# A row-tiled matmul with bias and residual: eight row tiles to a super tile, one listed order of transfers, and bf16 pairs transposed as words

## The chip, the cores and the metric

The kernel runs on one core of a Trainium2 chip. The metric is the device time of one execution in microseconds (us). Three runs of the kernel before gave a median of 217.84 us (216.41 to 219.18). The engines are named as in the profile: PE is TensorE's matmul stream and PEld its weight loads, DVE is VectorE, ACT is ScalarE, POOL is GpSimd, SP is SyncE, which issues nearly all transfers; a q behind a name (SPq, PEq) is that engine's queue of instructions.

## The reference

```python
batch, m, k, n = 16, 512, 1024, 768      # all float32
def reference(x, weight, bias, residual):
    return (np.matmul(x, weight) + bias + residual).astype(np.float32)
```

With the batch flattened it is one matmul of 8192 x 1024 by 1024 x 768, with a row of bias and a residual of the output's shape added. x is 33.6 MB, the residual and the output 25.2 MB each, the weight 3.1 MB: 87 MB to move.

## The kernel before, in words

**Tiling.** The 8192 rows are cut into 64 row tiles of 128 rows, and `J = 4` row tiles make a super tile S of 512 rows. Within a super tile, partition p holds J rows that follow each other in memory, so one transfer of x for a super tile is 2 MB, 16 KB in one piece for each partition; for the residual and the output it is 1.5 MB, 12 KB each. Row tile t is slice `t % 4` of super tile `t // 4`.

**One row tile** goes through these steps:

- `cast(t)` (L92): ACT turns the f32 x tile (128 x 1024) into the bf16 tile `xb`.
- `transp(t)` (L98 and L100): PE transposes the eight 128 x 128 blocks of `xb` into the PSUM tile `pt`, and DVE copies `pt` to `xt` in SBUF.
- `mm(t, k, n0, nl)` (L103): for each of the eight blocks k of the contraction and each of two column chunks (512 and 256) one bf16 matmul into the PSUM tile `psum_o`, 16 in all. Block k of W holds the rows 128k to 128k + 127.
- `finish(t)` and `pool_add(t)`: for the first eight tiles (`EARLY = 8`) DVE adds bias to the product into one of four `tmp` tiles (L122) and POOL adds that to the residual in `ro` (L114). For all later tiles POOL adds the bias to the residual row beforehand (L114), and DVE adds the product to that row (L124).

**Loop.** For t from 3 to 63 (L187), in program order: the cast of tile t + 2, at the last tile of a super tile the loads of x (S + 3), of the residual (S + 2) and the store of S - 1, the transposes of tile t + 1, the 16 matmuls of tile t, the finishing add of tile t - 1, and POOL's bias add of tile t + 1. Each engine keeps this order.

**Head.** `HEAD_ORDER` (L20) interleaves the loads of x tiles 0 to 2 and of the eight W chunks (each 128 x 768, 384 KB). When an x tile arrives it is cast, transposed and multiplied with the W chunks seen so far; when a W chunk arrives DVE casts it to bf16 (L164) and it is multiplied with the x tiles seen so far. Ahead of that stand eleven warming matmuls of 512 columns (L141), the load of the bias row on POOL's queue (L128), and two f32 matmuls of a row of ones with the bias row (L146) that spread the bias over the partitions, which DVE copies to `bias_sb` (L151).

**Buffers and queues.** x has three slots of a super tile, `ro` seven, of which the last two first hold the f32 W chunks. All loads and stores but the bias row's are issued by SP, in program order; one that waits for its slot or for its data holds up all behind it.

**Tail.** The last super tile is stored in parts: two row tiles, one, and the last one in its two column chunks, each after its own add (L205 to L212).

Of the kernel before, what the change touches and what calls it, by code (L numbers as in the profile page):

```python
# [19 lines left out]
HEAD_ORDER = [  # L20
    ("x", 0), ("w", 0), ("x", 1), ("w", 1), ("w", 2), ("x", 2),
    ("w", 3), ("w", 4), ("w", 5), ("w", 6), ("w", 7),
]


@with_exitstack
def kernel(
    ctx: ExitStack,
    tc: tile.TileContext,
    x: bass.AP,  # L30
    weight: bass.AP,
    bias: bass.AP,
    residual: bass.AP,
    out: bass.AP,
):
# [6 lines left out]
    n_k = K // P  # L42
# [9 lines left out]
    const = ctx.enter_context(tc.tile_pool(name="const", bufs=1))  # L52
# [3 lines left out]
    def ring(pool, name, i, n, shape, dt):  # L56
        return pool.tile(shape, dt, name=name, tag=f"{name}{i % n}", bufs=1)

    def psum_o(i):
        return ring(ps, "psum_o", i, HEAD, [P, N], FP32)  # L60

    x_sb, ro, xb, xt, po, tmp = {}, {}, {}, {}, {}, {}
    K_ = tc.keep_in_program_order

    def load_x(S, j0=0, j1=J):
        if S < n_s:
            if j0 == 0:
                x_sb[S] = ring(sb, "x_tile", S, X_BUFS, [P, J, K], FP32)
            K_(nc.sync.dma_start(out=x_sb[S][:, j0:j1, :], in_=x_d[S, :, j0:j1, :]))

    def load_res(S, j0=0, j1=J):
        if S < n_s:
            if j0 == 0:
                ro[S] = ring(sb, "ro", S, RO_BUFS, [P, J, N], FP32)
            K_(nc.sync.dma_start(out=ro[S][:, j0:j1, :], in_=res_d[S, :, j0:j1, :]))

    def store(S, j0=0, j1=J, n0=0, nl=N):
        if 0 <= S < n_s:
            K_(nc.sync.dma_start(
                out=out_d[S, :, j0:j1, n0:n0 + nl], in_=ro[S][:, j0:j1, n0:n0 + nl]  # L80
            ))

    w_st = [
        ring(sb, "ro", RO_BUFS - 2 + h, RO_BUFS, [P, n_k // 2, N], FP32) for h in range(2)
    ]
    w_sb = const.tile([P, n_k, N], BF16, name="w_sb")


    def cast(t):
        if t < n_t:  # L90
            xb[t] = ring(sb, "xb", t, 4, [P, K], BF16)
            K_(nc.scalar.copy(out=xb[t], in_=x_sb[t // J][:, t % J, :]))  # L92

    def transp(t):
        if t < n_t:
            pt = ring(ps, "pt", t, 2, [P, n_k, P], BF16)
            for k in range(n_k):
                K_(nc.tensor.transpose(out=pt[:, k, :], in_=xb[t][:, ts(k, P)], identity=ident))  # L98
            xt[t] = ring(sb, "xt", t, 4, [P, n_k, P], BF16)
            K_(nc.vector.tensor_copy(out=xt[t], in_=pt))  # L100

    def mm(t, k, n0, nl):
        K_(nc.tensor.matmul(  # L103
            po[t][:, n0:n0 + nl], lhsT=xt[t][:, k, :], rhs=w_sb[:, k, n0:n0 + nl],
            start=(k == 0), stop=(k == n_k - 1),
        ))

    def row(t, n0=0, nl=N):
        return ro[t // J][:, t % J, n0:n0 + nl]

    def pool_add(t):
        if t < n_t:
            r = row(t)
            K_(nc.gpsimd.tensor_add(out=r, in0=r, in1=tmp[t] if t < EARLY else bias_sb))  # L114

    def finish(t, n0=0, nl=N):
        if t < 0:
            return
        p = po[t][:, n0:n0 + nl]
        if t < EARLY:  # L120
            tmp[t] = ring(sb, "tmp", t, TMP_BUFS, [P, N], FP32)
            K_(nc.vector.tensor_add(out=tmp[t], in0=p, in1=bias_sb))  # L122
        else:
            K_(nc.vector.tensor_add(out=row(t, n0, nl), in0=p, in1=row(t, n0, nl)))  # L124


    bias_row = const.tile([1, N], FP32, name="bias_row")
    K_(nc.gpsimd.dma_start(out=bias_row, in_=bias[None, :]))  # L128
    warm = const.tile([P, 512], BF16, name="warm")
    K_(nc.vector.memset(warm, 0.0))  # L130
    ones_row = const.tile([1, P], FP32, name="ones_row")
    K_(nc.vector.memset(ones_row, 1.0))
    warm_a = const.tile([1, 2], FP32, name="warm_a")
    K_(nc.vector.memset(warm_a, 0.0))
    K_(nc.scalar.copy(out=warm_a, in_=warm_a))  # L135
    ident = const.tile([P, P], BF16, name="ident")
    make_identity(nc, ident)

    warm_ps = psum_o(0)
    for _ in range(WARM_MM):  # L140
        K_(nc.tensor.matmul(  # L141
            warm_ps[:, 0:512], lhsT=warm[:, 0:P], rhs=warm, start=True, stop=True
        ))
    bias_ps = psum_o(HEAD - 1)
    for n0, nl in chunks:
        K_(nc.tensor.matmul(  # L146
            bias_ps[:, n0:n0 + nl], lhsT=ones_row, rhs=bias_row[:, n0:n0 + nl],
            start=True, stop=True,
        ))
    bias_sb = const.tile([P, N], FP32, name="bias_sb")  # L150
    K_(nc.vector.tensor_copy(out=bias_sb, in_=bias_ps))  # L151


    seen_x, seen_w = [], []
    for kind, i in HEAD_ORDER:
        if kind == "x":
            load_x(0, i, i + 1)
            cast(i)
            transp(i)
            po[i] = psum_o(i)  # L160
            seen_x.append(i)
        else:
            K_(nc.sync.dma_start(out=w_st[i // 4][:, i % 4, :], in_=w_d[:, i, :]))
            K_(nc.vector.tensor_copy(out=w_sb[:, i, :], in_=w_st[i // 4][:, i % 4, :]))  # L164
            seen_w.append(i)
        for t in seen_x if kind == "w" else [i]:
            for k in [i] if kind == "w" else seen_w:
                for n0, nl in chunks:
                    mm(t, k, n0, nl)
    load_x(0, 3, 4)  # L170
    load_x(1, 0, 2)
    load_res(0, 0, 2)
    load_x(1, 2, 4)
    load_res(0, 2, 4)
    load_x(2)
    load_res(1)
    cast(HEAD)
    transp(HEAD)
    cast(HEAD + 1)
    load_x(3)  # L180
    load_res(2)
    for t in range(HEAD - 1):
        finish(t)
        pool_add(t)


    for t in range(HEAD, n_t):  # L187
        cast(t + 2)
        if (t + 2) % J == J - 1:
            S = (t + 2) // J  # L190
            load_x(S + X_BUFS)
            load_res(S + 2)
            store(S - 1)
        transp(t + 1)
        po[t] = psum_o(t)
        if t < n_t - 1:
            for k in range(n_k):
                for n0, nl in chunks:
                    mm(t, k, n0, nl)
# [5 lines left out]
    S = n_s - 1  # L205
    store(S, 0, J - 2)
    store(S, J - 2, J - 1)
    for n0, nl in chunks:
        for k in range(n_k):
            mm(n_t - 1, k, n0, nl)  # L210
        finish(n_t - 1, n0, nl)
        store(S, J - 1, J, n0, nl)  # L212


# [28 lines left out]
```

## Time and profile before

| what | value |
|---|---|
| three runs, median (lowest, highest) | 217.84 us (216.41, 219.18) |
| span of the profiled execution, first to last instruction | 216.1 us; the profile gives no time around it |
| mean granted TensorE clock | 0.975 of full speed |
| moved by DMA | 87.28 MB, mean 404 GB/s |
| HBM read, written | 61.87 MB, 25.17 MB |
| POOL waiting for residual loads | 60.8 us in 14 waits |
| ACT waiting for PE's transposes (slots of `xb`) | 102.8 us in 52 waits |
| ACT waiting for x loads | 24.2 us in 8 waits |

How to read it: the rows that the prediction quotes come from views of one profiled execution. The page shows each engine's busy time, and then the span in 40 equal slices (5.4 us each) with a digit of busy tenths. The chain that ended last lists start, duration and what was done. A group of instructions is a line, an engine, an operation and its operands, then the count, the busy time in us and the mean ns of one, then the idle time ahead of it and what ended that. A busy time of PE or PEld is not the distance from one instruction to the next, since they overlap. In the view by stretches, DMA share is the mean busy share of the core's 16 DMA engines, and the number ahead of it the granted clock.

### The profile page before, as it was taken

The page shows a single profiled execution, that of the slowest core. Times are in us where ns is not written, and L with a number is a line of the kernel's source. Part 1 is how long each engine was busy: PE and PEld are TensorE (multiplying, and loading weights), DVE is VectorE, ACT ScalarE, POOL GpSimd, SP SyncE. Part 2 cuts the span into 40 slices and gives each one's busy share as a digit, 9 for nine tenths or more (in the row PEclk, how much of TensorE's full clock was granted, in tenths as well). Part 3 has the DMA queues.
Part 4 walks back from the last instruction along what each step waited for, and adds up shares of the span by engine and source line. Part 5 has one row for each costly group of instructions (what it writes and reads, how often), then busy time and mean ns, then how long its engine had stood idle before and what let it go on. Part 6 is the DMA issues. An engine that isn't in the chain of part 4 may idle for free.

```text
span 216.1 us, 3672 instructions
## 1 busy us (share of the span) xinstructions
PE 205.2 (95%) x1551; PEld 132.4 (61%) x1551; DVE 105.1 (49%) x141; ACT 68.0 (31%) x66; POOL 115.3 (53%) x71
## 2 busy tenths in 40 slices
PE   7678799999999999999999999999999999999992
PEld 2335566666666666666666666666666666666651
DVE  0245365445554455445544555445544555445542
ACT  2314416323332333323332333323332333231000
POOL 2000096669928467390928457290936629099600
PEclk9658999999999999999999999999999999999999
DMA  6999999999999999999999999999999999999654
GB/s 179 393 413 418 441 413 429 428 425 431 428 422 431 425 427 421 434 422 421 440 418 436 426 432 420 431 428 422 434 417 438 421 432 424 434 414 416 260 233 176
DMA packets 9265, 87.28 MB, mean 404 GB/s; under 512 B 1056, under 2 KB 1184, under 8 KB 3360
## 3 DMA queue, kind: packets, MB, share of 16 engines
q1 hardware_dynamic: 9216, 87.04, 96.0%
q8 instruction: 12, 0.20, 0.4%
q14 instruction: 5, 0.04, 0.0%
q0 software_dynamic: 32, 0.00, 0.0%
HBM read 61.87 MB, written 25.17 MB: 403 GB/s over the span
## 4 chain that ended last, share of the span: by engine, by line
PE 93%; DVE 3%; DMA 3%; issue 1%; DVEq 0%; POOLq 0%
PE psum_o L103 78%; PE pt L98 13%; DMA bias_row<-in_bias_dram 3%; PE psum_o L146 1%; DVE xt L100 1%; DVE ro L124 1%; DVE tmp L122 0%; DVE bias_sb L151 0%; DVE w_sb L164 0%; DVEq L124 0%; DVEq L100 0%; POOLq L227 0%; POOLq masks.py:199 0%
## 5 line engine op out<-in xcount | busy, mean ns | idle before, releaser
L103 PE MATMUL psum_o<-w_sb,xt 128*128 128x256 bf16 (+1 forms) x1024 | 178.8, 328 | 4.9 <-DVE xt L100 1.6
L103 PEld LDWEIGHTS <-xt 128*128 128x128 bf16 x1024 | 97.8, 98 | 64.9 <-issue 2.2
L114 POOL TENSOR_TENSOR ro<-ro,bias_sb 128x768 f32<-128x768 f32 x56 | 99.7, 1812 | 59.5 <-DMA ro<-in_residual_dram 59.5
L92 ACT CAST xb<-x_tile 128x1024 bf16<-128x1024 f32 x64 | 66.5, 1046 | 127.0 <-PE pt L98 102.8
L100 DVE COPY xt<-pt 128x1024 bf16<-128x1024 bf16 x64 | 44.3, 692 | 94.6 <-PE pt L98 94.6
L124 DVE TENSOR_TENSOR ro<-psum_o,ro 128x768 f32<-128x768 f32 (+2 forms) x57 | 53.3, 935 | 4.9 <-PE psum_o L103 3.0
L98 PEld LDWEIGHTS <-xb 128*128 128x128 bf16 x512 | 34.9, 100 | 9.1 <-ACT xb L92 0.7
L98 PE MATMUL pt<-ident,xb 128*128 128x128 bf16 x512 | 40.1, 223 | 0.0
L114 POOL TENSOR_TENSOR ro<-ro,tmp 128x768 f32<-128x768 f32 x8 | 14.4, 1811 | 27.7 <-DVE tmp L122 26.3
L122 DVE TENSOR_TENSOR tmp<-psum_o,bias_sb 128x768 f32<-128x768 f32 x8 | 7.5, 948 | 0.0
L141 PE MATMUL psum_o<-warm 128*128 128x512 bf16 x11 | 3.9, 531 | 1.2 <-DVE warm L130 1.2
L151 DVE COPY bias_sb<-psum_o 128x768 f32<-128x768 f32 x1 | 1.0, 958 | 8.0 <-PE psum_o L146 8.0
L164 DVE CAST w_sb<-ro 128x768 bf16<-128x768 f32 x8 | 4.0, 553 | 0.0
L146 PE MATMUL psum_o<-bias_row,ones_row 1*128 1x512 f32 (+1 forms) x4 | 2.3, 720 | 1.7 <-DMA bias_row<-in_bias_dram 1.7
L141 PEld LDWEIGHTS <-warm 128*128 128x128 bf16 x11 | 1.3, 129 | 3.3 <-issue 1.9
L146 PEld LDWEIGHTS psum_o<-bias_row,ones_row 1*128 1x128 f32 x4 | 0.9, 234 | 3.0 <-issue 3.0
L135 ACT ACT_TABLE_LOAD x1 | 1.3, 1283 | 0.7 <-PEq L227 0.7
L128 POOL DMA_DIRECT2D bias_row<-in_bias_dram x1 | 0.6, 646 | 0.8 <-POOLq L227 0.8
L130 DVE MEMSET warm<- 128x256 uint32 x1 | 0.3, 272 | 0.9 <-PEq L227 0.9
masks.py:199 POOL TENSOR_SCALAR_AFFINE_SELECT ident<-ident 128x128 bf16<-128x128 bf16 x1 | 0.3, 292 | 0.1
L227 POOL MEMSET const-float32-0.0<- 128x1 f32 x1 | 0.1, 98 | 0.2 <-issue 0.2
masks.py:197 POOL MEMSET ident<- 128x128 bf16 x1 | 0.2, 224 | 0.0
(6 smaller groups left out, 0.7 us busy)
## 6 DMA issues: line engine op xcount, KB each, us to landing
x_tile<-in_x_dram SPq DMA_DIRECT2D x14, 2048.0 KB, 24.5
ro<-in_residual_dram SPq DMA_DIRECT2D x15, 1536.0 KB, 27.8
out_dram<-ro SPq DMA_DIRECT2D x15, 1536.0 KB, 25.3
ro<-in_weight_dram SPq DMA_DIRECT2D x8, 384.0 KB, 8.5
x_tile<-in_x_dram SPq DMA_DIRECT2D x4, 512.0 KB, 7.2
x_tile<-in_x_dram SPq DMA_DIRECT2D x2, 1024.0 KB, 11.2
ro<-in_residual_dram SPq DMA_DIRECT2D x2, 768.0 KB, 11.7
out_dram<-ro SPq DMA_DIRECT2D x1, 768.0 KB, 3.3
```

What stands on the lines that cost most here:

```text
L92: K_(nc.scalar.copy(out=xb[t], in_=x_sb[t // J][:, t % J, :]))
L98: K_(nc.tensor.transpose(out=pt[:, k, :], in_=xb[t][:, ts(k, P)], identity=ident))
L100: K_(nc.vector.tensor_copy(out=xt[t], in_=pt))
L103: K_(nc.tensor.matmul(po[t][:, n0:n0 + nl], lhsT=xt[t][:, k, :], rhs=w_sb[:, k, n0:n0 + nl], start=(k == 0), stop=(k == n_k - 1),))
L114: K_(nc.gpsimd.tensor_add(out=r, in0=r, in1=tmp[t] if t < EARLY else bias_sb))
L122: K_(nc.vector.tensor_add(out=tmp[t], in0=p, in1=bias_sb))
L124: K_(nc.vector.tensor_add(out=row(t, n0, nl), in0=p, in1=row(t, n0, nl)))
L135: K_(nc.scalar.copy(out=warm_a, in_=warm_a))
L141: K_(nc.tensor.matmul(warm_ps[:, 0:512], lhsT=warm[:, 0:P], rhs=warm, start=True, stop=True))
L146: K_(nc.tensor.matmul(bias_ps[:, n0:n0 + nl], lhsT=ones_row, rhs=bias_row[:, n0:n0 + nl], start=True, stop=True,))
L151: K_(nc.vector.tensor_copy(out=bias_sb, in_=bias_ps))
L164: K_(nc.vector.tensor_copy(out=w_sb[:, i, :], in_=w_st[i // 4][:, i % 4, :]))
```

## The change

Six things change together.

1. `J` goes from 4 to 8. A super tile is 1024 rows; a transfer of x is 4 MB (32 KB per partition), of the residual or output 3 MB (24 KB per partition).
2. All SBUF and PSUM tiles are made once, as lasting slots: two for x, four for the residual and output (`R`), four each for `xb` and `xt`. The f32 W chunks first use slot 1 of `R`, and the early tiles' temporary results slot 3.
3. All transfers but the bias row's stand in one list, `ORDER`. The function `pump` issues, on SP, each entry of the list as soon as the program has written the instructions that it depends on; it is called after every step that could allow one more. The order of the list is the order on SP.
4. W is laid out so that partition p of a pair chunk q holds the rows 256q + 2p and 256q + 2p + 1. The bf16 tile `xb` is read as f32 words, each a pair of neighbouring bf16 values; PE transposes four blocks of 128 x 128 words in place of eight of bf16, with an f32 identity. The matmuls then take every second bf16 element of `xt` as their weights. The number and shape of the matmuls stay.
5. The head is written out in `HEAD_ORDER`: the two casts of each pair of x tiles run on DVE and ACT, the two halves of each W chunk likewise, and each W chunk is multiplied with tiles 0 to 2 when it comes; tile 3 is transposed in the head too. There are 24 warming matmuls of 256 columns in three groups. The bias row is loaded by ACT's queue.
6. Only the first six tiles go through a temporary result, and POOL's adds follow a list `ADDS` for the first 16 tiles. The last tile's two column chunks go to two PSUM tiles, and it is stored in one transfer.

The diff, cut to its core:

```diff
-J = 4
+J = 8
+X_SLOTS = 2
+RO_SLOTS = 4
 HEAD = 3
-X_BUFS = 3
-RO_BUFS = 7
-TMP_BUFS = 4
-EARLY = 8
-WARM_MM = 11
+WARM = 10
+EARLY_END = 6
+TMP_SLOT = {0: 3}
+ADDS = [6, 0, 7, 8, 1, 9, 2, 10, 3, 11, 4, 12, 5, 13, 14, 15]
+HEAD_ORDER = [('bias',), ('warm', 10), ('cast', 0, 'v'), ('cast', 1, 's'), ('tr', 0), ('tr', 1),
+ ('wc', 0, 0, 's'), ('wc', 0, 1, 'v'), ('warm', 4), ('mm', 0, 0), ('mm', 1, 0),
+ ('cast', 2, 'v'), ('cast', 3, 's'), ('tr', 2), ('tr', 3), ('wc', 1, 0, 's'), ('wc', 1, 1, 'v'),
+ ('mm', 2, 0), ('mm', 0, 1), ('mm', 1, 1), ('mm', 2, 1), ('wc', 2, 0, 's'), ('wc', 2, 1, 'v'),
+ ('mm', 0, 2), ('mm', 1, 2), ('mm', 2, 2), ('wc', 3, 0, 's'), ('wc', 3, 1, 'v'),
+ ('cast', 4, 's'), ('mm', 0, 3), ('mm', 1, 3), ('mm', 2, 3)]
+ORDER = [('x', 0, 0, 2), ('w', 0, 0, 2), ('x', 0, 2, 4), ('w', 1, 0, 2), ('w', 2, 0, 2), ('w', 3, 0, 2),
+ ('x', 0, 4, 6), ('x', 0, 6, 8), ('r', 0, 0, 5), ('x', 1, 0, 4), ('r', 0, 5, 8), ('r', 1, 0, 5),
+ ('x', 1, 4, 8), ('x', 2, 0, 8), ('r', 1, 5, 8), ('r', 2, 0, 8), ('x', 3, 0, 8), ('s', 0, 0, 8),
+ ('r', 3, 0, 8), ('x', 4, 0, 8), ('r', 4, 0, 8), ('s', 1, 0, 8), ('x', 5, 0, 8), ('r', 5, 0, 8),
+ ('s', 2, 0, 8), ('x', 6, 0, 8), ('r', 6, 0, 8), ('s', 3, 0, 8), ('x', 7, 0, 8), ('r', 7, 0, 8),
+ ('s', 4, 0, 8), ('s', 5, 0, 8), ('s', 6, 0, 8), ('s', 7, 0, 5), ('s', 7, 5, 7),
+ ('s', 7, 7, 8)]
...
-    w_d = weight.rearrange("(ko ki) n -> ki ko n", ki=P)
+    w_d = weight.rearrange("(q p e) n -> p q e n", p=P, e=2)
...
+    XT = fixed(sb, "xt", XT_N, [P, n_q, P, 2], BF16)
+    PT = fixed(ps, "pt", 2, [P, n_q, P], FP32)
+    (ident,) = fixed(sb, "ident", 1, [P, P], FP32)
...
+    def pump():
+        while queue:
+            kind, S, j0, j1 = queue[0]
+            if kind == "w":
+                need = []
+            elif kind == "x":
+                need = [("cast", J * (S - X_SLOTS) + j) for j in range(j0, j1)] if S >= X_SLOTS else []
+            elif kind == "r":
+                need = [("store", S - RO_SLOTS, j) for j in range(j0, j1)] if S >= RO_SLOTS else []
...
+            else:
+                need = [("out", J * S + j) for j in range(j0, j1)]
+            if not all(n in done for n in need):
+                return
...
     def transp(t):
         if t < n_t:
-            pt = ring(ps, "pt", t, 2, [P, n_k, P], BF16)
-            for k in range(n_k):
-                K_(nc.tensor.transpose(out=pt[:, k, :], in_=xb[t][:, ts(k, P)], identity=ident))
-            xt[t] = ring(sb, "xt", t, 4, [P, n_k, P], BF16)
-            K_(nc.vector.tensor_copy(out=xt[t], in_=pt))
+            words = XB[t % XB_N].bitcast(FP32)
+            pt = PT[t % 2]
+            for q in range(n_q):
+                K_(nc.tensor.transpose(out=pt[:, q, :], in_=words[:, ts(q, P)], identity=ident))
+            K_(nc.vector.tensor_copy(
+                out=XT[t % XT_N].rearrange("p q m e -> p (q m e)"),
+                in_=pt.rearrange("p q m -> p (q m)").bitcast(BF16),
+            ))
...
+            PO[t % HEAD][:, n0:n0 + nl], lhsT=XT[t % XT_N][:, q, :, e],
+            rhs=w_sb[:, q, e, n0:n0 + nl],
...
-    K_(nc.gpsimd.dma_start(out=bias_row, in_=bias[None, :]))
+    K_(nc.scalar.dma_start(out=bias_row, in_=bias[None, :]))
...
     for t in range(HEAD, n_t):
         cast(t + 2)
-        if (t + 2) % J == J - 1:
-            S = (t + 2) // J
-            load_x(S + X_BUFS)
-            load_res(S + 2)
-            store(S - 1)
+        pool_adds(t + 1)
         transp(t + 1)
...
         finish(t - 1)
-        if t - 1 < EARLY:
-            pool_add(t - 1)
-        if t + 1 >= EARLY:
-            pool_add(t + 1)
+        pool_adds(t + 1)
```

More of the change, by code (lines that the diff above doesn't have):

```diff
@@ L77, in store, with fixed @@
[L77 to L89, printed above, removed]
-        if t < n_t:
-            xb[t] = ring(sb, "xb", t, 4, [P, K], BF16)
-            K_(nc.scalar.copy(out=xb[t], in_=x_sb[t // J][:, t % J, :]))
+    def fixed(pool, name, n, shape, dt):
+        return [pool.tile(shape, dt, name=f"{name}", tag=f"{name}{i}", bufs=1) for i in range(n)]
@@ new lines @@
+    X = fixed(sb, "x_tile", X_SLOTS, [P, J, K], FP32)
+    R = fixed(sb, "ro", RO_SLOTS, [P, J, N], FP32)
+    XB = fixed(sb, "xb", XB_N, [P, K], BF16)
+    XT = fixed(sb, "xt", XT_N, [P, n_q, P, 2], BF16)
+    PO = fixed(ps, "psum_o", HEAD, [P, N], FP32)
+    PT = fixed(ps, "pt", 2, [P, n_q, P], FP32)
+    (w_sb,) = fixed(sb, "w_sb", 1, [P, n_q, 2, N], BF16)
+    (bias_sb,) = fixed(sb, "bias_sb", 1, [P, N], FP32)
+    (bias_row,) = fixed(sb, "bias_row", 1, [1, N], FP32)
+    (ones_row,) = fixed(sb, "ones_row", 1, [1, P], FP32)
@@ L127, with tmp, pool_adds @@
-    bias_row = const.tile([1, N], FP32, name="bias_row")
-    K_(nc.gpsimd.dma_start(out=bias_row, in_=bias[None, :]))
-    warm = const.tile([P, 512], BF16, name="warm")
+        return R[t // J % RO_SLOTS][:, t % J, n0:n0 + nl]
+    def tmp(t):
+        return R[TMP_SLOT[t // J]][:, t % J, :]
+    adds = list(ADDS) + list(range(max(ADDS) + 1, n_t))
+    def pool_adds(upto):
+        for t in [t for t in adds if t <= upto]:
+            if ("r", t) not in done or (t < EARLY_END and ("fin", t) not in done):
+                return
+            adds.remove(t)
+            r = row(t)
+            if t < EARLY_END:
+                K_(nc.gpsimd.tensor_add(out=r, in0=r, in1=tmp(t)))
+                mark("add", t)
+                mark("out", t)
+            else:
+                K_(nc.gpsimd.tensor_add(out=r, in0=r, in1=bias_sb))
+                mark("add", t)
@@ L130, with finish @@
+    def finish(t):
+        p = PO[t % HEAD]
+        if t < EARLY_END:
+            K_(nc.vector.tensor_add(out=tmp(t), in0=p, in1=bias_sb))
+            mark("fin", t)
+        else:
+            assert ("add", t) in done, t
+            K_(nc.vector.tensor_add(out=row(t), in0=p, in1=row(t)))
+            mark("out", t)
+    K_(nc.scalar.dma_start(out=bias_row, in_=bias[None, :]))
     K_(nc.vector.memset(warm, 0.0))
-    ones_row = const.tile([1, P], FP32, name="ones_row")
     K_(nc.vector.memset(ones_row, 1.0))
-    warm_a = const.tile([1, 2], FP32, name="warm_a")
@@ L170, with bias_rows @@
[L170 to L181, printed above, removed]
+    for _ in range(WARM):
+        K_(nc.tensor.matmul(PO[0][:, 0:256], lhsT=warm[:, 0:P], rhs=warm, start=True, stop=True))
+    def bias_rows():
+        bias_ps = PO[HEAD - 1]
+        for n0, nl in chunks:
+            K_(nc.tensor.matmul(
+                bias_ps[:, n0:n0 + nl], lhsT=ones_row, rhs=bias_row[:, n0:n0 + nl],
+                start=True, stop=True,
+            ))
+        K_(nc.vector.tensor_copy(out=bias_sb, in_=bias_ps))
@@ new lines @@
+    pump()
+    for kind, *a in HEAD_ORDER:
+        if kind == "bias":
+            bias_rows()
+        elif kind == "cast":
+            cast(*a)
+        elif kind == "warm":
+            for _ in range(a[0]):
+                K_(nc.tensor.matmul(PO[1][:, 0:256], lhsT=warm[:, 0:P], rhs=warm, start=True, stop=True))
+        elif kind == "tr":
+            transp(a[0])
+        elif kind == "wc":
+            q, e, eng = a
+            copy = {"v": nc.vector.tensor_copy, "s": nc.scalar.copy, "g": nc.gpsimd.tensor_copy}[eng]
+            K_(copy(out=w_sb[:, q, e, :], in_=w_st[:, 2 * q + e, :]))
+            if (q, e) == (n_q - 1, 1):
+                mark("wcast", q)
+        else:
+            for e in range(2):
+                for n0, nl in chunks:
+                    mm(a[0], n0, nl, a[1], e)
@@ L200 @@
         finish(t - 1)
-        if t - 1 < EARLY:
-            pool_add(t - 1)
-        if t + 1 >= EARLY:
-            pool_add(t + 1)
[L205 to L212, printed above, removed]
+        pool_adds(t + 1)
+    t = n_t - 1
+    tail = [(PO[t % HEAD], 0, 512), (PO[(t - 2) % HEAD], 512, N - 512)]
+    for p, n0, nl in tail:
+        for q in range(n_q):
+            for e in range(2):
+                K_(nc.tensor.matmul(
+                    p[:, 0:nl], lhsT=XT[t % XT_N][:, q, :, e], rhs=w_sb[:, q, e, n0:n0 + nl],
+                    start=(q == 0 and e == 0), stop=(q == n_q - 1 and e == 1),
+                ))
+        K_(nc.vector.tensor_add(out=row(t, n0, nl), in0=p[:, 0:nl], in1=row(t, n0, nl)))
@@ L216 @@
+    mark("out", t)
+    pump()
+    assert not queue, queue
 _INS = ['x', 'weight', 'bias', 'residual']
```

113 lines of the change are left out of this document (44 added, 69 removed).

## The prediction

> **What bounds the kernel now.** I read the page first, then the chain that ended last, then the engines and the DMA by stretches of time. The page:
>
> ```profile
> span 216.1 us, 3672 instructions
> PE 205.2 (95%) x1551; PEld 132.4 (61%) x1551; DVE 105.1 (49%) x141; ACT 68.0 (31%) x66; POOL 115.3 (53%) x71
> ...
> PE   7678799999999999999999999999999999999992
> ...
> PEclk9658999999999999999999999999999999999999
> DMA  6999999999999999999999999999999999999654
> GB/s 179 393 413 418 441 413 429 428 425 431 428 422 431 425 427 421 434 422 421 440 418 436 426 432 420 431 428 422 434 417 438 421 432 424 434 414 416 260 233 176
> ...
> q1 hardware_dynamic: 9216, 87.04, 96.0%
> ```
>
> Two resources are full at once: PE in every slice from the sixth to the last but one, the DMA engines from the second to the 37th. The chain, in order of time (start, duration, what), says which sets the end:
>
> ```profile
> 18.77 6.02 PE psum_o L103 x36
> ...
> 26.89 2.77 PE psum_o L103 x16
> 29.67 0.45 PE pt L98 x8
> 30.11 2.60 PE psum_o L103 x16
> ...
> 206.38 0.45 PE pt L98 x8
> 206.82 4.34 PE psum_o L103 x24
> ...
> 212.00 1.05 PE psum_o L103 x8
> ```
>
> From 29.67 on it is PE without a hole: 0.45 us for 8 transposes (56 ns each) and 2.60 us for 16 matmuls, 3.05 us a row tile. 61 tiles (3 to 63) from 26.89 give 26.89 + 61 x 3.05 = 212.9, and the last matmuls do end at 213.05. So PE sets the end: head, plus 61 times the tile. Now the DMA by stretches (length, busy time of PE, PEld, DVE, ACT, POOL, granted clock, DMA share, GB/s):
>
> ```profile
> 24.00:196.00 172.00, 170.80 (x1352) 112.84 (x1350) 89.44 (x115) 60.37 (x58) 106.52 (x60) 1.00 1.01 427
> 196.00:216.10 20.10, 16.18 (x120) 10.19 (x118) 8.53 (x12) 0.00 (x0) 7.44 (x5) 0.99 0.63 259
> 0.00:24.00 24.00, 18.24 (x84) 9.42 (x85) 7.18 (x15) 7.64 (x8) 1.36 (x7) 0.79 0.93 358
> 6.89:9.25 2.36, 2.36 (x6) 0.94 (x7) 0.00 (x1) 1.04 (x1) 0.00 (x0) 0.62 1.04 416
> 8.00:11.40 3.40, 2.17 (x11) 1.09 (x9) 2.12 (x3) 0.97 (x1) 0.00 (x0) 0.50 1.02 405
> 16.00:20.00 4.00, 3.21 (x20) 1.93 (x19) 1.97 (x4) 1.04 (x1) 0.00 (x0) 0.79 1.02 422
> ```
>
> The first three move 73.4, 5.2 and 8.6 MB, 87.2 in all. At 427 GB/s that is 204.2 us. The head's 8.6 MB would take 20.1 us at that rate, so it loses 3.9; the tail's 5.2 MB would take 12.2, so it loses 7.9: 3.9 + 204.2 + 7.9 = 216.0, the span again. A faster PE can therefore win back the tail's 7.9 us and the head's 3.9 at most. Below that lies a DMA floor.
>
> **The change, by parts. Transposes.** This edit is in the diff alone: two bf16 values are taken as one f32 word, so a tile needs 4 transposes of 128x128 words in place of 8 of bf16, and its weight operand for the matmuls is every second element. No f32 transpose is in the trace. The nearest rows by form (busy us, mean ns):
>
> ```profile
> L103 PEld LDWEIGHTS <-xt 128*128 128x128 bf16 x1024 | 97.8, 98 | 64.9 <-issue 2.2 <-DVE xt L100 2.0 <-DVE w_sb L164 1.5
> L98 PE MATMUL pt<-ident,xb 128*128 128x128 bf16 x512 | 40.1, 223 | 0.0
> L98 PEld LDWEIGHTS <-xb 128*128 128x128 bf16 x512 | 34.9, 100 | 9.1 <-ACT xb L92 0.7 <-issue 0.6
> L146 PE MATMUL psum_o<-bias_row,ones_row 1*128 1x512 f32 x2 | 1.5, 813 | 1.7 <-DMA bias_row<-in_bias_dram 1.7
> L146 PE MATMUL psum_o<-bias_row,ones_row 1*128 1x256 f32 x2 | 1.1, 626 | 0.0
> L146 PEld LDWEIGHTS psum_o<-bias_row,ones_row 1*128 1x128 f32 x4 | 0.9, 234 | 3.0 <-issue 3.0
> ```
>
> Cheap end: a word costs what a bf16 element costs, 4 x 56 ns = 0.22 us a tile. Dear end: an f32 transpose costs what f32 arithmetic costs. The bias matmuls move 768 columns in the 2.36 us of the stretch 6.89:9.25 at clock 0.62, 1.46 us at full clock; by columns 128 take 0.24 us, some four times the bf16 transpose, so 4 cost 0.89 to 0.97 us, twice what is removed. Between them lies the weight load: f32 234 ns at clock 0.62 is 145 at full clock against 100 for bf16. As bf16 loads of 100 ns come every 56, they overlap; scaled alike, f32 loads come every 81 ns, 0.32 us for four. A transpose moves data and adds nothing up, so I hold the L98 rows for the nearest and take 0.30 us, a tile of 2.90. The step of two in the matmuls' weights costs nothing if the load stays under the 256-column matmul (2.60 us / 8 per pair, a third of it: 108 ns; the load shows 98); taking the f32 load's 145 ns for it, 37 x 8 = 0.30 us a tile. I take nothing.
>
> The Trainium skill, "TensorE: Matmul & The Clock Gate", Terms, says that weight loads and matmuls have a transpose mode four times faster for FP32. By that the price is the cheap end, 0.22 us; no run here shows it. The same page, "Weight-path perf modes", says that the fast weight load is not for FP32 but may be strided, and under "LDWEIGHTS" prices a plain load at columns over 1.2, 107 ns for 128. By that four transposes would cost 0.43 us, nearly what goes away; this is the first rival below.
>
> **Head.** In the trace, casts wait for these landings:
>
> ```profile
> 5.66 1.04 ACT L92 CAST xb<-x_tile 128x1024 bf16<-128x1024 f32 x1 [3.44 <-DMA x_tile<-in_x_dram]
> ...
> 17.69 1.04 ACT L92 CAST xb<-x_tile 128x1024 bf16<-128x1024 f32 x1 [5.10 <-DMA x_tile<-in_x_dram]
> ...
> L92 ACT CAST xb<-x_tile 128x1024 bf16<-128x1024 f32 x64 | 66.5, 1046 | 127.0 <-PE pt L98 102.8 <-DMA x_tile<-in_x_dram 24.2
> L164 DVE CAST w_sb<-ro 128x768 bf16<-128x768 f32 x8 | 4.0, 553 | 0.0
> ```
>
> At 17.69 x tiles 0 to 3 and all of W had landed, 5.24 MB. The new list asks for the same 5.24 MB first, so the last W chunk lands at about 17.7. Its halves are cast side by side, 0.55 us on DVE and about 0.78 (1046 x 768/1024) on ACT, then 12 matmuls (1.95 us): 20.4. PE then transposes tile 4, whose 1.05 MB of x lands 2.5 us after 17.7, 20.2, and is cast by 21.3; tile 3's matmuls start at 21.6 instead of 26.89. If the clock stays at the 0.50 of 8.00:11.40 until some 18 us (16 to 20 shows a mean of 0.79), the 48 head matmuls (7.8 us at full clock) fall behind and it is about 22.7. I take 21.6, 5.3 us gained on PE. Transfers of x in pairs and W in 6 KB runs should trim the head's DMA loss; bounds 2.7 and 3.9, I take 3.4.
>
> The bias row goes past GpSimd to the ScalarE queue; ScalarE idles 3.44 us there, which covers an issue of 0.4 us. The warm matmuls (24 of 256 columns for 11 of 512) lie in time when PE waits for x; without that cover they would cost at most 24 x 0.21 = 5 us at half clock.
>
> **First adds.** Rows by form, and the queue:
>
> ```profile
> L114 POOL TENSOR_TENSOR ro<-ro,bias_sb 128x768 f32<-128x768 f32 x56 | 99.7, 1812 | 59.5 <-DMA ro<-in_residual_dram 59.5
> L124 DVE TENSOR_TENSOR ro<-psum_o,ro 128x768 f32<-128x768 f32 x55 | 52.2, 949 | 3.0 <-POOL ro L114 1.9 <-PE psum_o L103 1.1
> L100 DVE COPY xt<-pt 128x1024 bf16<-128x1024 bf16 x64 | 44.3, 692 | 94.6 <-PE pt L98 94.6
> SPq L79 <- DVE ro L124: 97.8, 17, 11.8
> out_dram<-ro SPq DMA_DIRECT2D x1, 128.0 KB, 1.7
> L79 SPq DMA_DIRECT2D out_dram<-ro x19: 332/343/348, 34.1 to 213.5; - x19
> ```
>
> POOL's list begins with tile 6, whose residual is the 11th entry (12.6 MB: 3.4 + 29.5 = 33 us), and then takes turns between an early tile and a later one: 3.62 us for two adds where PE makes a tile in 2.90. DVE's add waits for POOL, and behind it on DVE stands the next tile's copy (0.69 us), for which PE waits. Six tiles with 0.72 us too much each, less about 2 us of lead: PE loses 2 us around 40 to 60 us, unseen while the DMA is the limit.
>
> **Order and slots.** All transfers stand in one list on SP; each waits in it, with all behind it, for its slot. Stores wait in SP now for 97.8 us in total without starving the DMA, since loads are queued ahead. In the new list x of super tile S needs the casts of S-2, and the residual of S+4 the store of S. Adding up bytes at 427: x4 reaches the DMA at about 87 us, its slot is free at about 76 (tile 23's cast); every later entry has its condition met 5 us or more before its turn, up to s6. The last loads end at 3.4 + 74.5 MB/0.427 = 178, and stores 4 to 7 follow. s7's first part starts at 200.2, its last 0.39 MB at 206.7. PE ends at 21.6 + 61 x 2.90 + 2 = 200.5, the last add by 201.7: 5 us before its store's turn. So the DMA never stops.
>
> **Sum.** 3.4 lost at the start + 204.2 + what follows the last byte. The last store is issued at 213.5 and lands 1.7 later, of which 0.3 is transfer; half the rest, 0.7 by estimate, comes after the last byte, and the span ends 0.9 later (216.1): 1.6. Together 209.2 us, 6.9 less than the profiled span. The page has no time around the span; the runs shown (216.41 to 219.18) stand 0.3 to 3.1 above it, their median 1.7. Taking 6.9 off the median 217.84: **210.9 us**. PE is the limit again from 21.6 + 61p + 3.2 = 206.7, a tile p of 2.98 or 95 ns a transpose.
>
> The Trainium skill, "DMA: Bandwidth & Descriptors", "Where 436 GB/s comes from", puts the ports at 435 GB/s; the trace's 427 is close, and at 435 the sum would be 205.5.
>
> **Rivals.**
> 1. *Weight loads no longer hide.* A transposed tile costs the same 0.45 us as before, or the stepped weights cost 0.30. For: the f32 load's 234 ns. Against: loads overlap, 100 ns every 56. PE ends at 21.6 + 61 x 3.05 + 1 = 208.7, last add 1.2, store 1.4 + 0.9, end 0.9: 213.1, so 214.8 (with 1.7 for the median, as above). The Trainium skill, "TensorE: Matmul & The Clock Gate", "LDWEIGHTS", would make it so.
> 2. *f32 transposes at arithmetic's price* (the slower side). 0.89 us a tile, 3.49: 21.6 + 212.9 + the same 1.2 + 2.3 + 0.9 = 238.9, so 240.6. For: the only f32 rows on PE are four times dearer per column. It decides over the head's gain from 21.6 + 61p + 4.4 = 216.1, p = 3.12, 130 ns a transpose.
> 3. *The transfers run slower*: x in runs of 32 KB with all reads far apart, or holes where SP waits. At 8.00:11.40's 405 GB/s: 3.4 + 215.3 + 1.6 = 220.3, so 222; halfway, 216.4. Against: nothing between 24 and 196 us changes with the tile.
> 4. *The list brings nothing at the head* because of the cold clock: 1.1 us on PE, inside PE's 5 us of slack, so still 210.9.
>
> **How the numbers follow.** Forecast with rival 4: 0.66. Rival 1: 0.15, rival 2: 0.12, rival 3: 0.07. Two per cent, about what a measurement of this kernel can tell from no change, is 213.5 and 222.2. The forecast is faster in nearly all of its chance, rival 1 in a fifth; rival 2 is slower but for prices near 130 ns; rival 3 mostly within. Faster 0.68, same 0.20, slower 0.12. Low end: 432 GB/s, as in single slices, takes 2.3 off, the head's bound 0.7, the lowest run 1.4: 206.5. High end 216.5 holds rival 1 with its scatter.
>
> **What would show it.** Right: transposes of a tile under 0.38 us in the chain; GB/s at about 427 to the last slice; the chain ending in DMA or SP instead of PE; tile 3's matmuls at 21 to 23 us. Wrong: PE unbroken in the chain with 0.43 us or more for 4 transposes (rival 1 or 2); slices below 420 between 24 and 190 us (rival 3).

## The result, and the profile after

The changed kernel takes 211.38 us (four runs, 211.29 to 211.41) where the kernel before took 218.49 beside it: a ratio of 0.972, with a 95% interval of 0.9654 to 0.9785. The forecast was 210.9 in a range of 206.5 to 216.5. Measured again, beside the first experiments, it took 211.28 against 216.72, 0.9736 (0.9698 to 0.9774). Times are medians; one of the six executions of the kernel with the bias row on GpSimd's queue took 553.86 us, the profiled one, and is left out here with its profile. The span of the profiled execution is 209.6 us, its own time 211.39, so 1.8 lie around the span. The number came out nearly as forecast. The mechanism did not, as the page shows at once (row by row: PE and DMA busy in 40 slices of the span, GB/s, and the chain that ended last by engine):

```profile
span 209.6 us, 3135 instructions
...
PE   7999999999999999999999999999999999999992
...
DMA  6999999999999999999999999999999999999785
GB/s 236 425 434 436 427 403 448 456 406 404 462 450 402 417 441 425 421 458 400 436 458 422 425 403 436 446 441 419 427 427 446 425 413 435 432 419 441 336 379 231
...
PE 97%; DVE 1%; issue 0%
```

PE is full from the second slice on and has 97% of the chain; the DMA is full to the 37th slice, as before, but the three half-empty slices behind are fuller (7, 8 and 5 tenths instead of 6, 5 and 4). The chain in order of time (start, duration, what):

```profile
1.05 2.32 PE psum_o L191 x10
3.37 2.85 PE psum_o L196 x4
6.22 2.25 PE psum_o L210 x10
8.47 1.71 PE pt L139 x8
10.17 0.85 PE psum_o L210 x4
11.03 1.90 PE psum_o L146 x8
12.93 0.45 PE pt L139 x4
...
14.15 6.75 PE psum_o L146 x40
20.90 0.44 PE pt L139 x4
21.34 2.60 PE psum_o L146 x16
...
200.50 2.60 PE psum_o L146 x16
203.10 2.61 PE psum_o L244 x16
...
205.74 0.42 DVE ro L248
```

A row tile is still 3.04 us: 2.60 for 16 matmuls and 0.44 for the four f32 transposes, where eight bf16 ones took 0.45. What changed is the start. Tile 3's matmuls begin at 21.34 instead of 26.89, 5.55 us earlier; the 61 tiles from there to the last matmul take 184.4 us instead of 186.2, and what follows it 3.9 instead of 3.05: -5.55 - 1.8 + 0.85 = -6.5, the whole difference of the spans. Part of the 1.8 is the wait between the two column chunks of the last tile, which now lie in two PSUM tiles: 0.85 us before, none now. The profiled execution of the kernel before took 217.84 us, about one more than its medians beside the experiments (216.72 to 216.90), so about one of the 6.5 may be scatter of that kernel, and these profiles do not say where it lies.

The stretches of time (columns as in the prediction; the last two are DMA share and GB/s):

```profile
0.00:24.00 24.00, 22.59 (x115) 14.22 (x116) 10.30 (x18) 10.88 (x12) 0.70 (x6) 1.00 0.94 387
24.00:196.00 172.00, 172.00 (x1135) 113.40 (x1134) 89.19 (x114) 57.16 (x56) 113.85 (x64) 1.00 1.01 430
```

The head moves 387 GB/s instead of 358, the middle 430 instead of 427, and between 24 and 196 us PE is busy for 172.00 of 172.00 us.

### The profile page after: what moved, and what is told of

It is laid out like the page before. It is cut to its first block, busy times and chain, and to the rows that moved or that the text cites. A ratio compares the mean times of both kernels' runs of the same rounds, so it can differ in the third digit from the quotient of the medians.

```text
span 209.6 us, 3135 instructions
## 1 busy us (share of the span) xinstructions
PE 204.3 (97%) x1308; PEld 133.6 (64%) x1308; DVE 104.7 (50%) x139; ACT 68.0 (32%) x68; POOL 114.6 (55%) x70
## 4 chain that ended last, share of the span: by engine, by line
PE 97%; DVE 1%; issue 0%
PE psum_o L146 79%; PE pt L139 14%; PE psum_o L210 1%; PE psum_o L196 1%; PE psum_o L244 1%; PE psum_o L191 1%; DVE xt L140 0%; DVE ro L248 0%; DVE warm L185 0%
## 5 line engine op out<-in xcount | busy, mean ns | idle before, releaser
L146 PE MATMUL psum_o<-w_sb,xt 128*128 128x512 bf16 x1008 | 174.7, 327 | 0.3 <-DVE xt L140 0.3
L171 POOL TENSOR_TENSOR ro<-ro,bias_sb 128x768 f32<-128x768 f32 x58 | 103.2, 1818 | 53.5 <-DMA ro<-in_residual_dram 53.5
L131 ACT CAST xb<-x_tile 128x1024 bf16<-128x1024 f32 x62 | 63.2, 1044 | 116.4 <-PE pt L139 58.6
L181 DVE TENSOR_TENSOR ro<-psum_o,ro 128x768 f32<-128x768 f32 x57 | 54.2, 950 | 12.0 <-POOL ro L171 10.9
L139 PE MATMUL pt<-ident,xb 128*128 128x128 f32 x256 | 39.0, 277 | 0.0
L139 PEld LDWEIGHTS pt<-ident,xb 128*128 128x128 f32 x256 | 30.7, 143 | 7.3
L167 POOL TENSOR_TENSOR ro<-ro 128x768 f32<-128x768 f32 x6 | 10.8, 1814 | 25.2 <-DMA ro<-in_residual_dram 25.2
L177 DVE TENSOR_TENSOR ro<-psum_o,bias_sb 128x768 f32<-128x768 f32 x6 | 5.6, 950 | 3.5 <-PE psum_o L146 3.5
L216 ACT CAST w_sb<-ro 128x768 bf16<-128x768 f32 x4 | 3.3, 832 | 3.8 <-DMA ro<-in_weight_dram 3.8
L210 PE MATMUL psum_o<-warm 128*128 128x256 bf16 x14 | 3.4, 416 | 0.0
L191 PE MATMUL psum_o<-warm 128*128 128x256 bf16 x10 | 2.3, 418 | 1.1 <-DVE warm L185 1.1
```

Source lines behind the costliest of these rows:

```text
L131: K_((nc.scalar.copy if how == "s" else nc.vector.tensor_copy)(out=dst, in_=src))
L139: K_(nc.tensor.transpose(out=pt[:, q, :], in_=words[:, ts(q, P)], identity=ident))
L146: K_(nc.tensor.matmul(PO[t % HEAD][:, n0:n0 + nl], lhsT=XT[t % XT_N][:, q, :, e], rhs=w_sb[:, q, e, n0:n0 + nl], start=(q == 0 and e == 0) ...
L167: K_(nc.gpsimd.tensor_add(out=r, in0=r, in1=tmp(t)))
L171: K_(nc.gpsimd.tensor_add(out=r, in0=r, in1=bias_sb))
L177: K_(nc.vector.tensor_add(out=tmp(t), in0=p, in1=bias_sb))
```

## The experiments

Three questions were open: what a packed transpose costs and why, what sets the end now, and which parts brought the 5.5 us at the head.

**Control.** The changed kernel, unaltered.

> The changed kernel again, unaltered, as the measure for the others on this chip. Expected 211.4 us, as before, a span of 209.6 and an unbroken PE in the chain from about 14 us on.

211.28 us (211.0 to 211.76), span 209.5; tile 3's matmuls start at 20.96 here, so two profiles of one kernel lie 0.4 us apart at this point. All that follows is compared with 211.28. The control, the bf16 transposes, the kernel without warming matmuls and the first with half of the transposes ran on one chip, the others on another, where the changed kernel was not run unaltered; the kernel before took 216.72 us on the one and 216.90 and 216.72 on the other, so differences of a few tenths between the two groups mean little.

**Eight bf16 transposes again.**

```diff
-            for q in range(n_q):
-                K_(nc.tensor.transpose(out=pt[:, q, :], in_=words[:, ts(q, P)], identity=ident))
+            for k in range(2 * n_q):
+                K_(nc.tensor.transpose(out=pt[:, k, :], in_=XB[t % XB_N][:, ts(k, P)], identity=ident))
...
-    w_d = weight.rearrange("(q p e) n -> p q e n", p=P, e=2)
+    w_d = weight.rearrange("(q e p) n -> p q e n", p=P, e=2)
```

> The changed kernel with eight bf16 transposes a tile in place of four of packed words (W rows in the layout of before, two runs of 3 KB per pair chunk). Theory A: PE is the limit in both kernels and the packed transposes bring next to nothing (0.44 us a tile against 0.45), the gain being PE's earlier start: 60 tiles x 0.013 = 0.8 us more, 212.2 us, tile pitch 3.05. Theory B, the prediction's: the packed transposes carry a large part of the gain: 214 us or more.

212.07 us (211.87 to 212.25), 0.8 more, as theory A has it; the matmuls of two tiles of its chain start at 33.54 and 36.59, 3.05 apart. Up to 33.54 its chain runs through the landing of tile 8's x at 31.72; in the two profiles of the changed kernel the same matmuls start at 33.48 and 33.11, so up to 0.4 of the 0.8 may come from that landing and not from the pitch. The packing is worth 0.8 of the gain at most, and the theory on which the forecast stood falls.

**What a packed transpose costs.** Groups of 32 PE instructions behind the last tile, such as

```diff
+    for i in range(32):
+        K_(nc.tensor.transpose(out=PT[0][0:64, 1, :], in_=words[:, 0:64], identity=ident))
+    for i in range(32):
+        K_(nc.tensor.transpose(out=PT[0][:, 2, 0:64], in_=words[0:64, 0:P], identity=ident[0:64, 0:64]))
```

> The changed kernel, and behind its last tile eight groups of 32 PE instructions with 4 matmuls of 256 columns between: f32 transposes of 128x128 words; the same with 64 word columns as weights; the same with 64 columns moving; bf16 transposes of 128x128; bf16 matmuls of 128 columns with packed weights; with every second element as weights; matmuls of 64 columns with stepped and with packed weights. Theory L (the f32 weight load sets the pitch): full 109 ns, 64 weight columns 55, 64 moving 109. Theory M (f32 words move at two cycles a column): full 109, 64 weight columns 109, 64 moving 55. Theory S (load and move one after the other): both halves 80. bf16 transposes 56; matmuls of 128 columns 56 packed and stepped alike if the stepped load hides.

PE's order of time behind the last tile (start, busy time, line, operands, partitions and columns of weights, moving operand, count). In a transpose the block of x is the weights, and the identity moves. From one group's start to that of the 4 matmuls after it is 32 pitches:

```profile
206.66 3.66 PE L262 MATMUL pt<-ident,xb 128*128 128x128 f32 x32
210.16 0.60 PE L258 MATMUL psum_o<-warm 128*128 128x256 bf16 x4
210.59 3.66 PE L265 MATMUL pt<-ident,xb 128*64 128x128 f32 x32
214.09 0.60 PE L258 MATMUL psum_o<-warm 128*128 128x256 bf16 x4
214.62 2.23 PE L268 MATMUL pt<-ident,xb 64*128 64x64 f32 x32
216.78 0.61 PE L258 MATMUL psum_o<-warm 128*128 128x256 bf16 x4
217.23 1.95 PE L272 MATMUL pt<-ident_b,xb 128*128 128x128 bf16 x32
219.01 0.60 PE L258 MATMUL psum_o<-warm 128*128 128x256 bf16 x4
219.45 1.95 PE L275 MATMUL psum_o<-w_sb,warm 128*128 128x128 bf16 x32
221.24 0.60 PE L258 MATMUL psum_o<-warm 128*128 128x256 bf16 x4
221.68 1.95 PE L278 MATMUL psum_o<-w_sb,xt 128*128 128x128 bf16 x32
223.46 0.60 PE L258 MATMUL psum_o<-warm 128*128 128x256 bf16 x4
223.90 1.10 PE L281 MATMUL psum_o<-w_sb,xt 128*128 128x64 bf16 x32
224.83 0.60 PE L258 MATMUL psum_o<-warm 128*128 128x256 bf16 x4
```

A full f32 transpose takes 3.50/32 = 109 ns. With half the weight columns it is 109 again; with half the moving columns (and half the rows) 2.16/32 = 67. So theories L and S fall. Theory M comes nearest: a column of the f32 identity takes twice the time of a bf16 one (1.78/32 = 56 ns for a full bf16 transpose). It has the first two groups right, but the third at 55 instead of 67; something else, the load perhaps, stands close behind, and that is not settled. Nor is it settled whether f32 in the moving operand alone would cost this, as the weights are f32 too. The f32 result in PSUM is not the cause, since the bf16 matmuls of L275 write f32 as well and come every 56 ns. Weights with a step of two (L278) take the same 56 ns as packed ones (L275), and with 64 moving columns (L281) 0.93/32 = 29 ns: the step is free here, as forecast.

**Half of the transposes.** The kernel leaves out two of the four word blocks of each tile and uses the other two twice.

```diff
-            for q in range(n_q):
+            for q in range(n_q // 2):
                 K_(nc.tensor.transpose(out=pt[:, q, :], in_=words[:, ts(q, P)], identity=ident))
...
-            PO[t % HEAD][:, n0:n0 + nl], lhsT=XT[t % XT_N][:, q, :, e],
+            PO[t % HEAD][:, n0:n0 + nl], lhsT=XT[t % XT_N][:, q // 2, :, e],
```

> Leaves out half of the transposes: two of the four word blocks are transposed and copied, and each is used twice as weights. PE's tile falls from 3.04 to 2.82 us, 13 us over the loop. Theory A (PE the limit now, a DMA floor a little below it): the DMA takes over, 87.2 MB at 430 GB/s after 2.4 us lost at the start and 1.6 at the end, span 206.8, time 208.6. Rival: the DMA keeps up a higher rate or is not the next limit: below 205, or no gain at all if POOL or the slots bind.

210.87 us (210.79 to 211.38), span 209.1. PE's tile falls to 2.82 us and its last matmul ends at about 197, 8.7 us earlier than in the changed kernel's first profile; the time falls by 0.4. Its chain is now mostly DMA:

```profile
DMA 50%; PE 34%; POOL 7%; issue 1%; DVE 1%; SPq 1%; ACT 1%; ACTq 0%; POOLq 0%
```

So a second limit lies 0.4 us below the first. It is the DMA, which still works for ten us after PE's end, though its floor is 209.1 in the span and not the 206.8 expected here. The last microseconds, by stretches (the last two numbers are DMA share and GB/s):

```profile
204.00:205.00 1.00, 0.00 (x0) 0.00 (x0) 0.00 (x0) 0.00 (x0) 0.00 (x0) 0.50 0.90 372
205.00:206.00 1.00, 0.00 (x0) 0.00 (x0) 0.00 (x0) 0.00 (x0) 0.00 (x0) 0.50 0.60 243
206.00:207.00 1.00, 0.00 (x0) 0.00 (x0) 0.00 (x0) 0.00 (x0) 0.00 (x0) 0.50 0.21 83
207.00:208.00 1.00, 0.00 (x0) 0.00 (x0) 0.00 (x0) 0.00 (x0) 0.00 (x0) 0.50 0.05 18
```

All stores have been issued by 198, yet the 16 engines do not finish together: their mean busy share falls from 0.90 to 0.60, 0.21 and 0.05, at the last about one engine in 16. They run out over some three microseconds, which a sum of bytes over a mean rate doesn't see.

**Half of the transposes, transfers of four tiles.** The same kernel, which leaves the same blocks out, with each 8-tile entry of the list cut in two:

```diff
-('x', 2, 0, 8)
+('x', 2, 0, 4), ('x', 2, 4, 8)
```

> The kernel with half of its transposes left out (so that the DMA sets the end), with each 8-tile transfer from super tile 2 on cut into two of 4 tiles: runs of 16 and 12 KB instead of 32 and 24. Theory A: run length above 12 KB brings nothing, the engines being full either way: within 0.5 us of the 210.9 of half transposes with 8-tile transfers. Theory B (longer runs raise the DMA's rate, 430 against 427 GB/s): 1.2 to 1.6 us more.

211.70 us (211.59 to 211.73), 0.8 more, between the two theories. Its row of the middle:

```profile
24.00:196.00 172.00, 166.81 (x1047) 105.47 (x1066) 77.32 (x119) 56.94 (x56) 113.84 (x64) 1.00 1.01 427
```

427 GB/s again, as in the kernel before, against 430 in the same stretch with 8-tile transfers. The larger transfers are worth about 0.8 us where the DMA sets the end; the two runs were on different chips. Whether the length of the runs in memory or the number of transfers does it was not told apart.

**No warming matmuls.**

```diff
-WARM = 10
+WARM = 0
```

The two `warm` entries of `HEAD_ORDER` go as well.

> The changed kernel without its 24 warming matmuls. Theory A1: the head gained because PE was kept busy and so came to full clock by 12 to 14 us instead of 18: without them tile 3 starts 2 to 4 us later, 213.5 to 215.5 us. Theory A2: the head gained by the order of landings and casts alone, the last W chunk setting its end: 211.4 us, give or take 0.3.

211.61 us (211.43 to 211.76), 0.3 more, where the control's own runs go up to 211.76. Theory A1 falls: the warming matmuls are not what brought PE forward. In PE's order of time the loop even starts earlier without them, at 20.32 instead of the control's 20.80. The lead is lost again before tile 8, whose x lands at 31.2, and the chain runs through that transfer. PE's last matmul still ends at 205.39, against 205.58 in the control; the 0.3 comes behind it, where the stores run out (4.4 us to the end against 3.9). The longest pieces of its chain begin:

```profile
1.16 6.11 DMA ro<-in_weight_dram
7.28 23.91 DMA x_tile<-in_x_dram
```

**The bias row on GpSimd's queue again.**

```diff
-    K_(nc.scalar.dma_start(out=bias_row, in_=bias[None, :]))
+    K_(nc.gpsimd.dma_start(out=bias_row, in_=bias[None, :]))
```

> The changed kernel with the bias row on GpSimd's queue again. Theory A (PE is the limit and the bias matmuls stand first in its order): the row lands at about 6.8 us instead of 3.3, all of PE's head moves 2 to 3 us, and the time to 213.3 to 214.3. Rival (the last W chunk sets the head, or the DMA floor hides it): 211.3, give or take 0.4.

214.1 us (214.02 to 214.33; ratio to the kernel before 0.9853, 0.9802 to 0.9903), 2.8 more, as theory A has it. This one line is the largest of the parts that were undone singly. In the chain of the kernel before one sees what it did there:

```profile
1.24 5.51 DMA bias_row<-in_bias_dram
...
6.89 2.34 PE psum_o L146 x4
```

Issued by GpSimd, the 3 KB take 5.51 us; issued by ScalarE at 0.73, in the kernel without warming matmuls, they release PE at 2.16.

**The same line alone, in the kernel before.**

> The kernel before with the bias row alone moved to the ScalarE queue. Theory A (the bias matmuls held PE's queue until 9.2 us): the first transposes start at 7 instead of 9.1, PE's loop 2 to 3 us earlier, 2 to 3 us less than the kernel before, about 214. Rival (the head is held by the W casts behind the third tile's copy and by the half clock): less than 0.7 us.

215.53 us against 216.9, a ratio of 0.9928 (0.9888 to 0.9968): 1.4 us, between the two. In its profile the bias matmuls begin at 5.64 instead of 6.89, and run in 1.50 us instead of 2.34, near the 1.46 that the prediction worked out for full clock; the head then ends as before behind the third tile's copy and the W casts:

```profile
5.64 1.50 PE psum_o L146 x4
...
16.49 6.02 PE psum_o L103 x36
```

36 matmuls begin at 16.49 instead of 18.77: all that follows is 2.3 us earlier, in the profiled executions 213.9 against 216.1 of span. The medians differ by 1.4 only, as the profiled execution of the kernel before was 0.9 us longer than its median here.

**Casts on one engine each.** All x casts of the head on ScalarE, all W casts on VectorE.

```diff
-('cast', 0, 'v'), ('cast', 1, 's')
+('cast', 0, 's'), ('cast', 1, 's')
...
-('wc', 0, 0, 's'), ('wc', 0, 1, 'v')
+('wc', 0, 0, 'v'), ('wc', 0, 1, 'v')
```

The later pairs alike.

> The changed kernel with all x casts of the head on ScalarE and all W casts on VectorE, as in the kernel before. Theory A: the last W chunk's second half is cast 0.3 to 0.6 us later and the first x pair 0.4 to 1 later, the loop starts 0.5 to 1 us later, 211.8 to 212.3 us. Rival: hidden by landings, 211.3.

211.80 us (211.51 to 211.93), 0.5 more, at the lower edge of theory A; the loop's first matmuls start at 21.61 against the control's 20.96. The unaltered kernel itself showed 20.96 and 21.34, so this is about the least that can be told here.

**Tile 3 transposed late.**

```diff
-('tr', 2), ('tr', 3), ('wc', 1, 0, 's')
+('tr', 2), ('wc', 1, 0, 's')
...
-('mm', 2, 3)]
+('mm', 2, 3), ('tr', 3)]
```

> The changed kernel with tile 3 transposed behind the head's last matmuls, as in the kernel before, instead of in the head. Theory A: its copy then stands ahead of the first finishing adds on VectorE, PE waits for the PSUM tile of tile 0, and tile 3's matmuls start at about 23.0 instead of 21.3: 1.3 to 1.7 us more, 212.6 to 213.0. Rival (the DMA floor or later slack takes it up): under 0.5 us more.

212.65 us (212.3 to 213.01), 1.4 more: theory A. Tile 3's matmuls start at 22.38, after the transposes, a copy and the first finishing add on VectorE: the wait that the kernel before had at 24.8 to 26.9.

**The last tile stored in two chunks.**

```diff
-    mark("out", t)
-    pump()
+        pump()
+        K_(nc.sync.dma_start(out=out_d[n_s - 1, :, J - 1:J, n0:n0 + nl],
+                             in_=R[(n_s - 1) % RO_SLOTS][:, J - 1:J, n0:n0 + nl]))
```

The last entry of `ORDER` goes.

> The changed kernel with the last row tile stored in its two column chunks, each after its own add. The last transfer is 128 KB instead of 384: 1.7 us to landing against 2.3 in the traces, 0.4 to 0.6 us less, 210.8. Rival (the DMA's own end, uneven over its engines, sets the end): 211.3.

211.26 us (211.07 to 211.72): nothing. Its last issue (KB, us to landing):

```profile
out_dram<-ro SPq DMA_DIRECT2D x1, 128.0 KB, 2.4
```

The 128 KB take 2.4 us to land instead of the 1.7 in the kernel before. That the DMA is still at work on what stands ahead would explain it; no run here isolates this.

**A candidate for a faster version**: no warming matmuls, the tail in two chunks (both as above), and x tiles 8 to 11 listed ahead of the first residual:

```diff
-('x', 0, 6, 8), ('r', 0, 0, 5), ('x', 1, 0, 4)
+('x', 0, 6, 8), ('x', 1, 0, 4), ('r', 0, 0, 5)
```

> The changed kernel without its warming matmuls, with x tiles 8 to 11 listed ahead of the first residual, and with the last row tile stored in two chunks. PE's loop starts about 1 us earlier and no longer waits for tile 8; the tail is 0.5 shorter. If PE alone sets the end: 209.8 us. If the DMA's end of about 208 in the span sets it too: 210.4 to 210.9.

215.37 us (214.79 to 216.96), 4.1 more. The chain from the residual to PE:

```profile
7.59 23.73 DMA ro<-in_residual_dram
...
31.46 7.11 POOL ro L166 x4
38.57 1.77 POOL ro L170
...
41.24 0.69 DVE xt L139
...
41.98 3.15 PE psum_o L145 x10
```

and the waits of VectorE and PE (total in us, times, longest):

```profile
DVE ro L180 <- POOL ro L170: 11.8, 5, 7.4
...
PE psum_o L145 <- DVE xt L139: 4.1, 2, 3.7
```

POOL's first add comes at 31.46 instead of 26.47, VectorE's add waits 7.4 us for POOL, the next tile's copy stands behind it, and PE waits 3.7 us; the ten matmuls after that take 315 ns each instead of 163, as the granted clock between 42 and 44 us is 0.50. Of the three edits the other two cost 0.3 and nothing by themselves, so most of the 4.1 comes with this order of transfers. The path (POOL, VectorE's add, the copy behind it, PE) is the one that the prediction described for the first adds. No version here that does all of the work beats the changed kernel.

## Why the prediction was right or wrong

**The transposes: wrong.** The step "I take 0.30 us, a tile of 2.90" failed. A packed transpose takes 109 ns, a tile 0.44 and 3.04. The reason given, that a transpose "adds nothing up" and so sides with the bf16 rows, does not hold: the f32 identity moves at half the speed of a bf16 one (109 against 56 ns). So it was neither the cheap nor the dear end, and not the number of weight columns, but about half of the 0.24 us worked out for f32 arithmetic. PE stayed unbroken in the chain with 0.44 us for four transposes, which the prediction had named as the sign of rival 1 or 2. The 107 ns of the Trainium skill ("TensorE: Matmul & The Clock Gate", "LDWEIGHTS") come near the 109, but by another cause, since half the weight columns change nothing. The transpose mode four times faster for FP32 (the Trainium skill, same page, Terms) is not borne out here: 109 ns is about half of the 0.24 us, not a quarter.

**The tile pitch at which PE is the limit again: condition met, its time missed.** The prediction gave 95 ns a transpose as the point from which PE binds; at 109 PE does bind, as rival 1 said. Rival 1's 213.1 of span came out as 209.6. Four reasons lie ahead of PE's end: the loop started at 21.34, not 21.6 (0.3); 1 us of stalls did not occur; the tile was 3.037, not 3.05 (0.8); and the last two tiles have no transposes behind them, so that 61 full tiles count two sets too many (0.9). That makes 205.7 for PE's end instead of 208.7. The formula had seemed to fit the kernel before, where the 0.85 us between the last chunks stood for the two transposes. What follows PE's end is 3.9 us, not 4.4.

**The DMA floor: right in sum, by chance.** 209.2 was forecast and 209.1 measured with half of the transposes gone. Its terms were off and made up for each other: 2.4 us lost at the start instead of 3.4, 430 GB/s instead of 427 (1.4 us less), and 3.9 us at the end instead of 1.6, since the engines do not finish together. That the forecast met the time of the changed kernel, though, is luck: PE sets its end, and happened to do so within 0.5 us of the DMA's. Rival 3's sign, slices below 420 GB/s between 24 and 190 us, does stand in the page (400 to 419 in ten slices), but three slices before had it too (413 to 418), and the mean rose from 427 to 430: a single slice is no measure of the rate.

**The head: right in time by luck, wrong in its path.** The start at 21.6 was 21.34. It was derived from the landing of W at 17.7 and of tile 4's x at 20.2, with the bias row's move as a cost covered by idle time. But both land two us earlier, as ScalarE's order of time shows; the last W cast and tile 4's cast begin as they land:

```profile
15.54 0.83 ACT L216 CAST w_sb<-ro 128x768 bf16<-128x768 f32 x1 [1.05 <-DMA ro<-in_weight_dram]
18.11 1.99 ACT L131 CAST xb<-x_tile 128x1024 bf16<-128x1024 f32 x2 [1.74 <-DMA x_tile<-in_x_dram]
```

What sets the start is PE's own order, which the chain follows from its first warming matmul at 1.05 to 21.34 with one wait for a copy, PE running at half speed for about half of that time. What the cold clock (rival 4) cost there was not measured apart; and the warming matmuls are not all covered by waits, as the loop starts 0.5 us earlier without them. The runs show that the bias row's move is worth 2.8 us, tile 3's early transposes 1.4 and the casts on two engines 0.5; with the packing's 0.8 these come to 5.5, where 216.72 and 211.28 differ by 5.4; parts undone singly overlap, so the agreement proves little, and the list of transfers as a whole was not undone. The bias matmuls stand ahead of the transposes in PE's order, so the landing of 3 KB held all of these; the rows for that (5.51 and 6.89 above) were in the profile and were not used.

**First adds: the path exists, but the list was misread.** No stall of 2 us came; PE waited for VectorE's copies 0.3 us in all, while VectorE waited for POOL 10.9 us in nine waits. POOL does not begin with tile 6: `pool_adds(upto)` passes over all tiles beyond `upto`, so the adds come out as 0, 1, 2, 3, 6, 4, 7, 5, 8. POOL's order of time (L167 adds an early tile's temporary result, L171 the bias) begins with four early adds at 26.47 instead of about 33, and takes turns for two pairs only, not for six tiles:

```profile
26.47 7.14 POOL L167 TENSOR_TENSOR ro<-ro 128x768 f32<-128x768 f32 x4 [25.16 <-DMA ro<-in_residual_dram]
34.09 1.81 POOL L171 TENSOR_TENSOR ro<-ro,bias_sb 128x768 f32<-128x768 f32 x1 [0.48 <-DMA ro<-in_residual_dram]
35.86 1.81 POOL L167 TENSOR_TENSOR ro<-ro 128x768 f32<-128x768 f32 x1
```

The candidate, whose first residual lands 5 us later, shows the same path closing at 4 us.

**Order and slots: right.** The DMA stays full from 24 to 196 us, and SP's in-order waits open no hole until the last stores.

## What to carry to other kernels

When two limits lie as close as here, work out both ends with their last microseconds before crediting a gain to one part, and test the second limit by leaving work of the first one out. Look at what stands first in the busiest engine's order: a transfer of 3 KB ahead of the first transposes was worth more here (2.8 us) than any other part that was undone. Packing two bf16 values into one f32 word halved the number of transposes but hardly PE's time for them (0.44 against 0.45 us a tile). And trace a list through the code that reads it before pricing its order.

## What the runs showed of the hardware that was not expected

- A PE transpose of f32 words comes every 109 ns for 128 moving columns, one of bf16 elements every 56; the number of f32 weight columns (64 or 128) does not matter, and a step of two elements in bf16 weights is free (56 and 56 ns).
- The granted clock in the profile reads 1.00 from the start, but the warming matmuls at 6.22 take 225 ns for 256 columns, and the transposes at 8.47 take 214 ns; from 12.93 on they take 112 (0.45 for four), and matmuls of 256 columns behind the last tile 108 (0.43 for four). So PE ran at half speed until some time between 11 and 13 us, and the clock column did not show it. Without warming matmuls it is much the same: eight transposes keep PE busy for 1.94 us from 6.80 on, and the next eight for 1.08 from 11.86 on.
- With the queue full to the last, the 16 DMA engines run dry over some 3 us (mean busy share 0.90, 0.60, 0.21, 0.05 in the last four).
- A row of 3 KB issued by GpSimd at the start took 5.51 us to land; issued by ScalarE it had landed 1.4 us after its issue began.
- After PE had waited 3.7 us in the candidate, its granted clock was 0.50 for the next two us.
